# Neighbourhood attention: scores as four 64x64 tiles with 24 key columns each, instead of two 64x128 tiles with up to 32

## The chip, the cores and the metric

One core of a Trainium2 chip. The metric is the device time of one execution in microseconds. The kernel before takes 1035.6 us (median of three runs, 1035.43 to 1036.15).

## The reference

An encoder layer on 2048 tokens of width 1024, in float32: RMSNorm, one projection to q, k, v and a gate, neighbourhood attention, a SiLU gate, an output projection, the residual, and a final RMSNorm. The tokens form a grid of 32 rows by 64 columns; there are 16 heads of 64. Each query sees a window of 8 rows by 16 columns, clipped at the borders of the grid, with a learned bias per head and relative position. Cut to the attention:

```python
def row_fn(r):
    rs = jnp.clip(r - kh // 2, 0, rows - kh)
    qr = ...            # queries of row r, in blocks of 16 columns
    kr = ...            # keys of rows rs .. rs+7, 32 columns to a block
    s = jnp.einsum('bnqhd,bknjhd->bhnqkj', qr, kr) * scale
    s = jnp.where(col_valid[None, None], s + bias[None], NEG_INF)
    p = jax.nn.softmax(s.reshape(B, H, nb, NA_QBLOCK, kh * NA_KBLOCK), axis=-1)
    o = jnp.einsum('bhnqkj,bknjhd->bnqhd', p, vr)
```

## The kernel before

The program has one order, written out by hand; the order in which calls stand is the order on each engine. Stages one and two do the norm and most of the projections, by seven products instead of eight, with every float32 operand split in two parts (`h` and `l`, float32r). From about 573 to 929 us runs the attention, and after it the rest of the output projection (`rows_by_seven`).

The attention has 32 steps and one more for what is left over. A step is a pair of heads `p` and a row block `T` of 8 grid rows (512 queries); the list `order` has all eight pairs for `T` = 0, then `T` = 1 and 2 by turns, then all pairs for `T` = 3. The keys of a block are 11, 15, 15 and 12 grid rows (`KEY_ROWS`). The 512 queries are cut into four tiles `C` of 128: 8 rows by 16 columns, in two halves of 64 queries (8 rows by 8 columns). Tile `C` has its keys in strips of 8 columns. `KEY_COLS` gives three strips (24 columns) to the tiles at the edges, `C` = 0 and 3, and four strips (32 columns) to the inner ones. A half, by itself, reaches only three strips (its own and one on each side), and two at an edge of the grid.

In step `m` TensorE gets, one after another:

- `feed`: projection or output-projection matmuls, so many per step (`amount`), which fill the time of the other engines (L384, L386, L388; later L1481, L1483, L1485);
- `turns(m - 1)`: 44 transposes of 64 queries by one strip each (L1258, `ph`) of the normalised scores of the step before, into six PSUM banks that ACT and DVE copy to SBUF, three each (L1234, `pta`);
- `scores(2m)` and `scores(2m + 1)`: for each `C` two matmuls, one per head (L1173, `s`). The heads of a pair lie on 64 partitions each, so the two use different row halves of the array and different banks. Then, per `C` and head, DVE adds bias and mask and takes the row minimum (L1181), ACT takes the exponential and its sum (L1187), and `normalise` scales by the reciprocal on POOL (L1201), or on ACT for the last tile (L1199);
- `values(2m - 2)` and `values(2m - 1)`: 28 matmuls (L1280, `o`), one per `C`, strip and head, with the two heads on different column halves of the array.

All PSUM tiles come from one ring of eight banks. `strips(C)` lists for each strip which halves need it, and `places`, `turns` and `values` go by it, so strips of a half that sees nothing there are neither transposed nor multiplied with values.

The bias of a tile is a table per head: `load_e` loads a row of 15 x 32 positions per query, and `bias` adds the mask on POOL or DVE (L1141, `em`). For `T` = 3 the sum is made ahead and `load_last` loads it (L1156).

Of the kernel before, what the change touches and what calls it, by code (L numbers as in the profile page):

```python
# [10 lines left out]
F32 = mybir.dt.float32  # L11
F32R = mybir.dt.float32r
BF16 = mybir.dt.bfloat16
# [19 lines left out]
PLAIN = 6  # L33

KEY_ROWS = [(0, 11), (4, 19), (12, 27), (20, 32)]
KEY_COLS = [(0, 24), (8, 40), (24, 56), (40, 64)]
ROW_TYPE = [0, 1, 1, 2]
COL_TYPE = [0, 1, 1, 2]
TYPE_ROWS = [(0, 11), (-4, 11), (-4, 8)]
TYPE_COLS = [(0, 24), (-8, 24), (-8, 16)]  # L40
MASK_N = [[(u1 - u0) * (v1 - v0) for v0, v1 in TYPE_COLS] for u0, u1 in TYPE_ROWS]
MASK_ALL = sum(sum(n) for n in MASK_N[:2])
LAST_ALL = sum(MASK_N[2])
KINDS = {"q": 0, "k": 4, "v": 8, "g": 12}


def mask_table():
    out = []
    for t, (u0, u1) in enumerate(TYPE_ROWS):
        T = (0, 1, 3)[t]  # L50
        for c, (v0, v1) in enumerate(TYPE_COLS):
            C = (0, 1, 3)[c]
            half, qr, col, strip, kr, kc = np.ogrid[:2, T * 8:T * 8 + 8, :8, :(v1 - v0) // 8, T * 8 + u0:T * 8 + u1, :8]
            qc = C * 16 + half * 8 + col
            kc = C * 16 + v0 + strip * 8 + kc
            rs = np.clip(qr - KH // 2, 0, ROWS - KH)
            cs = np.clip(qc - KW // 2, 0, GW - KW)
            ok = (kr >= rs) & (kr < rs + KH) & (kc >= cs) & (kc < cs + KW)
            out.append(np.where(ok, 0.0, NEG).astype(np.float32).reshape(128, -1))
    return np.concatenate(out, axis=1)  # L60


def strips(C):
    out = []
    for s in range(KEY_COLS[C][0] // 8, KEY_COLS[C][1] // 8):
        halves = [h for h in range(2) if abs(2 * C + h - s) <= 1]
        out.append((s, s - KEY_COLS[C][0] // 8, halves[0] * 64, len(halves) * 64))
    return out


# [1 line left out]
def build(ctx, tc, x, xr, xt, wg, rpb, last, w_out, n0, nf, masks, out):  # L72
# [55 lines left out]
        nc.tensor.matmul(zp, z[:, :128], z, start=True, stop=True)  # L128
    ident = one.tile([128, 128], F32, name="ident")
    make_identity(nc, ident)  # L130
    ones = one.tile([128, 128], F32, name="ones")
    nc.vector.memset(ones, 1.0)
    onesr = one.tile([128, 128], F32R, name="onesr")
# [950 lines left out]
    def slot(T, p):  # L1084
        return 7 if p == lastp[T] else p - (p > lastp[T])

    def width(C):
        return KEY_COLS[C][1] - KEY_COLS[C][0]

    def load_k(p, T):  # L1090
        r0, r1 = KEY_ROWS[T]
        n = (r1 - r0) * GW
# [30 lines left out]
    def load_e(p, ty, pool_=None, homes=None):  # L1123
        r0, r1 = (4, 15) if ty == 0 else (0, 15)

        def rows(s):
            t = (homes[s] if homes else (pool_ or ep)([128, 512], F32, "e"))[:, :480]
            E[p, s] = t.rearrange("p (u v) -> p u v", v=32)
            nc.sync.dma_start(t[:, r0 * 32:r1 * 32], rpb[2 * p + s][:, r0 * 32:r1 * 32])

        return [lambda: rows(0), lambda: rows(1)]

    def bias(p, ty, cty):
        m0 = sum(sum(n) for n in MASK_N[:ty]) + sum(MASK_N[ty][:cty])
        (u0, u1), (v0, v1) = TYPE_ROWS[ty], TYPE_COLS[cty]
        n = MASK_N[ty][cty]
        sh = lambda a: a.rearrange("p (s u v) -> p s u v", u=u1 - u0, v=8)
        for s in range(2):
            t = mp([128, 512], F32, "em")[:, :n]
            EM[p, ty, cty, s] = t  # L1140
            (nc.gpsimd if attending[0] or not s else nc.vector).tensor_tensor(  # L1141
                sh(t), E[p, s][:, u0 + 4:u1 + 4, v0 + 8:v1 + 8].rearrange("p u (s v) -> p s u v", v=8), sh(MK[0][:, m0:m0 + n]), OP.add)

    def load_last(p):
        if p % 2:
            ts = [mp([128, 512], F32, "em") for _ in range(6)]
        else:
            m = mkp([128, 1536], F32, "em")
            e = [ep([128, 512], F32, "em") for _ in range(2)]
            ts = [m[:, :288], m[:, 288:576], m[:, 576:960], m[:, 960:1344], e[0], e[1]]  # L1150
        fs = []
        at = 0
        for cty, n in enumerate(MASK_N[2]):
            for s in range(2):
                EM[p, 2, cty, s] = t = ts.pop(0)[:, :n]
                fs.append(lambda t=t, a=at, n=n, s=s: nc.sync.dma_start(t, last[2 * p + s, :, a:a + n]))  # L1156
            at += n
        return fs

# [2 lines left out]
    def scores(i, between=None):  # L1162
        p, T, cs = pairs[i]
        kt, qt = KT[p, T], QT[p, T]
        r0, r1 = KEY_ROWS[T]
        got = []
        for C in cs:
            c0, c1 = KEY_COLS[C]
            qs = slice(C * 128, C * 128 + 128)
            pst = [bank((r1 - r0) * (c1 - c0), f"s{s}") for s in range(2)]  # L1170
            for s in range(2):
                a = slice(s * 64, s * 64 + 64)
                nc.tensor.matmul(pst[s], qt[a, qs], kt[a, :r1 - r0, c0:c1].rearrange("p r (s c) -> p s r c", c=8), start=True, stop=True)  # L1173
            got.append((C, pst))
        ST[i] = st = tiny.tile([128, 12], F32, name="st")
        for j, (C, pst) in enumerate(got):
            n = (r1 - r0) * width(C)
            X[i, C] = [xp([128, 512], F32, f"x{s}")[:, :n] for s in range(2)]
            for s in range(2):
                o = 2 * j + s  # L1180
                nc.vector.tensor_tensor_reduce(X[i, C][s], pst[s], EM[p, ROW_TYPE[T], COL_TYPE[C], s], -1.0, 1e38,  # L1181
                                               OP.add, OP.min, st[:, o:o + 1])
            if between and j == 0:
                between()
            for s in range(2):
                o = 2 * j + s
                nc.scalar.activation(X[i, C][s], X[i, C][s], AF.Exp, bias=st[:, o:o + 1], scale=-1.0,  # L1187
                                     accum_out=st[:, 4 + o:5 + o])
# [12 lines left out]
                    nc.gpsimd.tensor_scalar(X[i, C][s], X[i, C][s], st[:, o:o + 1], 1.0, op0=OP.mult, op1=OP.mult)  # L1201

    def split(C):
        return [b for b in strips(C) if b[3] == 128], [b for b in strips(C) if b[3] == 64]

    def places(m):
        p, T = order[m]
        put, at = {}, [1024, 1024]  # L1210
        for C in range(4):
            full, part = split(C)
            for b, blk in enumerate(full):
                for s in range(2):
                    for h in range(2):
                        put[C, blk[0], s, h] = C * 256 + b * 128 + s * 64
            for blk in part:
                for s in range(2):
                    h = blk[2] // 64
                    put[C, blk[0], s, h] = at[h]  # L1220
                    at[h] += 64
        return put

    def turns(m):
        p, T = order[m]
        k = 8 * (KEY_ROWS[T][1] - KEY_ROWS[T][0])
        put = places(m)
        PT[m] = t = pt([128, 3072], F32, "pta").rearrange("p (h c) -> p h c", h=2)
        banks_ = {}

        def copy(b):
            w = (512, 512, 384)[b]
            for h in range(2):
                (nc.vector.tensor_copy if h else lambda o, i_: nc.scalar.activation(o, i_, AF.Copy))(  # L1234
                    t[:k, h, b * 512:b * 512 + w], banks_[b, h][:k, :w])

        for b in range(2):
            for h in range(2):
                banks_[b, h] = bank(512, f"ph{h}")
            if b == 0:  # L1240
                banks_[2, 0], banks_[2, 1] = bank(384, "ph0"), bank(384, "ph1")
            lists = [[], []]
            for C in (2 * b, 2 * b + 1):
                full, part = split(C)
                for blks in (full, part):
                    for blk in blks:
                        for s in range(2):
                            for h in range(2):
                                if (C, blk[0], s, h) in put:
                                    lists[h].append((put[C, blk[0], s, h], C, s, blk[1] * k))  # L1250
            for h in range(2):
                lists[h].sort()
            for n in range(max(len(l) for l in lists)):
                for h in range(2):
                    if n < len(lists[h]):
                        o, C, s, at = lists[h][n]
                        q = slice(64 * h, 64 * h + 64)
                        nc.tensor.transpose(banks_[o // 512, h][:k, o % 512:o % 512 + 64], X[2 * m + b, C][s][q, at:at + k], ident[q, q])  # L1258
                if n == 7:
                    copy(b)  # L1260
        copy(2)

    def values(i):
# [8 lines left out]
        for C in cs:  # L1272
            X.pop((i, C))
            full, part = split(C)
            for b, (strip, _, q0, nq) in enumerate(full + part):
# [557 lines left out]
```

## Time and profile before

| | |
|---|---|
| median of 3 runs | 1035.6 us |
| profiled execution, its own time | 1035.7 us |
| its span | 1033.9 us |
| TensorE matmul busy | 1022.7 us, 99% of the span |
| weight loads | 838.6 us, 81% |
| DVE / ACT / POOL busy | 768.7 / 557.5 / 263.6 us |
| DMA | 221.04 MB, 214 GB/s on average |
| TensorE clock granted | 0.997 |
| score matmuls (L1173) | 512, 95.2 us busy |
| reductions (L1181) | 256, 123.0 us busy |

In rows of the profile, PE is TensorE's matmuls and PEld its weight loads, which run beside them. A row of the groups or of the timeline names the line, the operation, output and inputs, and the shapes; `64*128 64x480` on a matmul is 64 rows of the array by 128 of its columns, with 480 columns streamed through. The start of a matmul is measured, its end is modelled. The chain of waits lists the work that ended last, step by step, with start and duration. In a row of the windows, each engine has its busy time and, in brackets, its number of instructions.

### The profile page before, as it was taken

To read this page: it belongs to the slowest core of one execution; us is meant where nothing else is said; L and a number is where in the kernel's file an instruction comes from. 1 tells how busy PE (TensorE), PEld (TensorE's weight loads), DVE (VectorE), ACT (ScalarE), POOL (GpSimd) and SP (SyncE) were. 2 spreads that over 40 slices of the span, in tenths; PEclk is the share of its full clock that TensorE was granted. 3 is DMA by queue.
4 is the path that set the end of the run, shared out by engine and by line. 5 is a ranking of instruction groups with operands and counts; after the bars stand their busy time and mean duration, and the time that the engine had idled before them with its cause. 6 is when DMAs were issued, how large, how long until landed. Compare 5 with 4: busy or idle time off the path is not lost.

```text
span 1033.9 us, 20333 instructions
## 1 busy us (share of the span) xinstructions
PE 1022.7 (99%) x7208; PEld 838.6 (81%) x7208; DVE 768.7 (74%) x1650; ACT 557.5 (54%) x1305; POOL 263.6 (25%) x352
## 2 busy tenths in 40 slices
PE   9999999999999999999999999999999999999997
PEld 7888888887888888888888788888878788888875
DVE  5476878989898866776775756587787797777875
ACT  7645324353344423343343677688788778673432
POOL 0000231221221000000002467756566423321010
PEclk9999999999999999999999999999999999999998
DMA  9634667655636755755567788688776599899553
GB/s 315 234 102 140 191 179 244 187 194 170 204 99 201 250 152 164 222 189 179 193 205 237 215 236 244 199 250 290 237 246 225 177 300 315 255 349 372 134 153 102
DMA packets 143902, 221.04 MB, mean 214 GB/s; under 512 B 13176, under 2 KB 61560, under 8 KB 143800
## 3 DMA queue, kind: packets, MB, share of 16 engines
q1 hardware_dynamic: 141928, 216.72, 66.5%
q0 software_dynamic: 1440, 2.62, 1.6%
q8 instruction: 57, 0.93, 0.4%
q14 instruction: 45, 0.37, 0.1%
q10 hardware_dynamic: 432, 0.40, 0.1%
HBM read 154.68 MB, written 65.01 MB: 212 GB/s over the span
## 4 chain that ended last, share of the span: by engine, by line
PE 95%; DVE 3%; ACT 1%; issue 1%; DMA 0%; SPq 0%; DVEq 0%; ACTq 0%
PE pp L440 37%; PE py L1563 9%; PE pv L564 8%; PE s L1173 8%; PE o L1280 8%; PE pv L956 7%; PE ph L1258 4%; PE pp L386 2%; PE po L1481 2%; PE pp L388 2%; PE pp L384 2%; PE po L1483 2%; PE po L1485 2%; DVE f L423 1%; DVE x L1181 0%
## 5 line engine op out<-in xcount | busy, mean ns | idle before, releaser
L440 PE MATMUL pp<-h,f 128*128 128x512 f32 x672 | 217.3, 389 | 0.0
L1187 ACT ACTIVATE x<-x,st 128x360 f32<-128x360 f32 (+5 forms) x256 | 151.2, 592 | 24.3 <-DVE st L1181 24.3
L440 PEld LDWEIGHTS pp<-h,f 128*128 128x128 f32 x672 | 126.1, 188 | 26.1
L440 PE MATMUL pp<-t,f 128*128 128x512 f32 x558 | 141.7, 389 | 0.1
L1201 POOL TENSOR_SCALAR x<-x,st 128x480 f32<-128x480 f32 (+5 forms) x192 | 114.4, 613 | 93.9 <-DVE st L1192 91.5
L440 PE MATMUL pp<-l,f 128*128 128x512 f32 x336 | 130.7, 389 | 0.0
L460 POOL TENSOR_TENSOR tmp<-tmp,rb 128x512 f32<-128x512 f32 x36 | 59.0, 1640 | 267.6 <-DVE tmp L458 231.3
L1181 DVE CUSTOM_DVE_ANT_0 x<-s,em 128x360 f32<-128x360 f32 (+5 forms) x256 | 123.0, 535 | 0.8 <-PE s L1173 0.8
L440 PEld LDWEIGHTS pp<-t,f 128*128 128x128 f32 x558 | 104.7, 188 | 22.3 <-DVE u L453 0.6
L1141 POOL TENSOR_TENSOR em<-e,mk 128x264 f32<-128x264 f32 (+3 forms) x64 | 50.8, 824 | 248.4 <-DMA mk<-in_masks_dram 234.8
L423 DVE TENSOR_TENSOR f<-raw,f 128x512 fp32r<-128x512 f32 x105 | 75.2, 716 | 28.9 <-ACT f L422 28.5
L1173 PE MATMUL s<-kt,q 64*128 64x480 f32 (+5 forms) x512 | 95.2, 487 | 0.1
L1280 PEld LDWEIGHTS o<-pta,vt 120*64 120x64 f32 (+2 forms) x1792 | 80.9, 137 | 14.4 <-DVE st L1181 13.6
L1280 PE MATMUL o<-pta,vt 120*64 120x128 f32 (+5 forms) x1792 | 85.5, 253 | 0.5 <-DVE pta L1234 0.4
L422 ACT ACTIVATE f<-raw 128x512 fp32r<-128x512 f32 x105 | 63.6, 622 | 31.6 <-DMA raw<-in_wg_dram 13.9
L1173 PEld LDWEIGHTS s<-kt,q 64*128 64x128 f32 x512 | 65.1, 186 | 15.8 <-DVE pta L1234 1.9
L1234 DVE COPY pta<-ph 120x512 f32<-120x512 f32 (+5 forms) x96 | 56.9, 639 | 24.2 <-PE ph L1258 24.0
L440 PEld LDWEIGHTS pp<-l,f 128*128 128x128 f32 x336 | 63.1, 188 | 13.2
L1234 ACT ACTIVATE pta<-ph 120x512 f32<-120x512 f32 (+5 forms) x96 | 49.8, 557 | 37.4 <-PE ph L1258 36.6
L422 ACT ACTIVATE f<-s 128x512 fp32r<-128x512 f32 x42 | 26.3, 625 | 53.2 <-DVE s L429 49.5
L440 PE MATMUL pp<-sixths,f 128*128 128x512 f32 x198 | 54.6, 389 | 0.0
L1258 PEld LDWEIGHTS ph<-ident,x 64*120 64x120 f32 (+2 forms) x1408 | 42.5, 128 | 11.3 <-issue 8.5
(213 smaller groups left out, 1995.2 us busy)
## 6 DMA issues: line engine op xcount, KB each, us to landing
raw<-in_wg_dram SPq DMA_DIRECT2D x120, 256.0 KB, 5.0
row<-in_xr_dram SPq DMA_DIRECT2D x32, 256.0 KB, 5.7
vd<-v SPq DMA_DIRECT2D x32, 256.0 KB, 4.4
sgd<-sg SPq DMA_DIRECT2D x32, 256.0 KB, 2.8
q<-qd SPq DMA_DIRECT2D x32, 256.0 KB, 5.3
sgt<-sgd SPq DMA_DIRECT2D x32, 256.0 KB, 6.0
ogd<-og SPq DMA_DIRECT2D x32, 256.0 KB, 3.8
kt<-kd SPq DMA_DIRECT2D x16, 480.0 KB, 6.0
```

The lines of the kernel that those rows point to most:

```text
L422: nc.scalar.activation(t[:, 0], src, AF.Copy)
L423: nc.vector.tensor_tensor(t[:, 1], src, t[:, 0].bitcast(F32), OP.subtract)
L440: nc.tensor.matmul(B[n, P], t[:, int(m == 2), c], x[k][int(m == 1)], start=P in (1, 6, 5) and k == 0 and m == 0, stop=k == 3 and m == 2, s ...
L564: nc.tensor.matmul(ps[t], a[:, o], b, start=k == 0 and m == 0, stop=k == NK - 1 and m == 2)
L1173: nc.tensor.matmul(pst[s], qt[a, qs], kt[a, :r1 - r0, c0:c1].rearrange("p r (s c) -> p s r c", c=8), start=True, stop=True)
L1181: nc.vector.tensor_tensor_reduce(X[i, C][s], pst[s], EM[p, ROW_TYPE[T], COL_TYPE[C], s], -1.0, 1e38, OP.add, OP.min, st[:, o:o + 1])
L1187: nc.scalar.activation(X[i, C][s], X[i, C][s], AF.Exp, bias=st[:, o:o + 1], scale=-1.0, accum_out=st[:, 4 + o:5 + o])
L1201: nc.gpsimd.tensor_scalar(X[i, C][s], X[i, C][s], st[:, o:o + 1], 1.0, op0=OP.mult, op1=OP.mult)
L1234: (nc.vector.tensor_copy if h else lambda o, i_: nc.scalar.activation(o, i_, AF.Copy))(t[:k, h, b * 512:b * 512 + w], banks_[b, h][:k, :w])
L1258: nc.tensor.transpose(banks_[o // 512, h][:k, o % 512:o % 512 + 64], X[2 * m + b, C][s][q, at:at + k], ident[q, q])
L1280: nc.tensor.matmul(to.rearrange("d (h q) -> d h q", q=64) if nq > 64 else to, vt[:k, strip, s * 64:s * 64 + 64], t[:k, h, at:at + 64] if n ...
L1563: nc.tensor.matmul(B[m, P], t[:, a, c], b, start=P in (1, 6, 5) and k == 0 and i == 0, stop=k == 3 and i == 2, skip_group_check=True)
```

## The change

Every score tile becomes 24 key columns wide, counted from the half's own left neighbour strip. For each `C` and head there are now two matmuls, one per half of 64 queries, with the output on partitions 0 to 63 or 64 to 127 of the same bank. At the two edges of the grid one of the three strips does not exist: the matmul there has 16 columns, and a small bf16 matmul of zeros fills the other 8, so that the mask can work on defined numbers. The order in a `C` is: half 0 of head 0, half 0 of head 1, half 1 of head 0, half 1 of head 1, with a half's zeros ahead of it.

Masks, bias tables and the sums for `T` = 3 follow: 24 columns everywhere, the same three kinds of tile (left edge, inner, right edge). Reductions, exponentials and normalisation have 264, 360 or 288 elements for all tiles, where inner ones had 352, 480 or 384. Transposes and values keep their number and size and read at other offsets. The table loads have 24 columns instead of 32.

```diff
+    zeros = one.tile([128, 128], BF16, name="zeros")
+    nc.vector.memset(zeros, 0.0)
...
 def strips(C):
     out = []
-    for s in range(KEY_COLS[C][0] // 8, KEY_COLS[C][1] // 8):
+    for s in range(max(2 * C - 1, 0), min(2 * C + 3, 8)):
         halves = [h for h in range(2) if abs(2 * C + h - s) <= 1]
-        out.append((s, s - KEY_COLS[C][0] // 8, halves[0] * 64, len(halves) * 64))
+        out.append((s, halves[0] * 64, len(halves) * 64))
     return out
...
         for C in cs:
-            c0, c1 = KEY_COLS[C]
-            qs = slice(C * 128, C * 128 + 128)
-            pst = [bank((r1 - r0) * (c1 - c0), f"s{s}") for s in range(2)]
-            for s in range(2):
-                a = slice(s * 64, s * 64 + 64)
-                nc.tensor.matmul(pst[s], qt[a, qs], kt[a, :r1 - r0, c0:c1].rearrange("p r (s c) -> p s r c", c=8), start=True, stop=True)
+            pst = [bank((r1 - r0) * 24, f"s{s}") for s in range(2)]
+            R = (r1 - r0) * 8
+            for h in range(2):
+                g = 2 * C + h
+                j0, j1 = max(1 - g, 0), min(9 - g, 3)
+                q = slice(h * 64, h * 64 + 64)
+                for s in range(2):
+                    a = slice(s * 64, s * 64 + 64)
+                    if j1 - j0 < 3:
+                        j = 0 if j0 else 2
+                        nc.tensor.matmul(pst[s][q, j * R:j * R + R], zeros[a, :64], zeros[a, :R], start=True, stop=True)
+                for s in range(2):
+                    a = slice(s * 64, s * 64 + 64)
+                    nc.tensor.matmul(pst[s][q, j0 * R:j1 * R], qt[a, C * 128 + h * 64:C * 128 + h * 64 + 64],
+                                     kt[a, :r1 - r0, 8 * (g - 1 + j0):8 * (g - 1 + j1)].rearrange("p r (s c) -> p s r c", c=8),
+                                     start=True, stop=True)
             got.append((C, pst))
...
-            n = (r1 - r0) * width(C)
+            n = (r1 - r0) * 24
...
-            t = (homes[s] if homes else (pool_ or ep)([128, 512], F32, "e"))[:, :480]
+            t = (homes[s] if homes else (pool_ or ep)([128, 512], F32, "e"))[:, :360]
...
-                sh(t), E[p, s][:, u0 + 4:u1 + 4, v0 + 8:v1 + 8].rearrange("p u (s v) -> p s u v", v=8), sh(MK[0][:, m0:m0 + n]), OP.add)
+                sh(t), E[p, s][:, u0 + 4:u1 + 4].rearrange("p u (s v) -> p s u v", v=8), sh(MK[0][:, m0:m0 + n]), OP.add)
...
-                                lists[h].append((put[C, blk[0], s, h], C, s, blk[1] * k))
+                                lists[h].append((put[C, blk[0], s, h], C, s, (blk[0] - 2 * C - h + 1) * k))
```

More of the change, by code (lines that the diff above doesn't have):

```diff
@@ L35 @@
 KEY_ROWS = [(0, 11), (4, 19), (12, 27), (20, 32)]
-KEY_COLS = [(0, 24), (8, 40), (24, 56), (40, 64)]
 ROW_TYPE = [0, 1, 1, 2]
@@ L39 @@
 TYPE_ROWS = [(0, 11), (-4, 11), (-4, 8)]
[L40 to L43, printed above, removed]
+MASK_N = [(u1 - u0) * 24 for u0, u1 in TYPE_ROWS]
+MASK_ALL = 3 * sum(MASK_N[:2])
 KINDS = {"q": 0, "k": 4, "v": 8, "g": 12}
@@ L50, in mask_table @@
         T = (0, 1, 3)[t]
-        for c, (v0, v1) in enumerate(TYPE_COLS):
-            C = (0, 1, 3)[c]
-            half, qr, col, strip, kr, kc = np.ogrid[:2, T * 8:T * 8 + 8, :8, :(v1 - v0) // 8, T * 8 + u0:T * 8 + u1, :8]
+        for C in (0, 1, 3):
+            half, qr, col, strip, kr, kc = np.ogrid[:2, T * 8:T * 8 + 8, :8, :3, T * 8 + u0:T * 8 + u1, :8]
             qc = C * 16 + half * 8 + col
-            kc = C * 16 + v0 + strip * 8 + kc
+            kc = C * 16 + half * 8 - 8 + strip * 8 + kc
             rs = np.clip(qr - KH // 2, 0, ROWS - KH)
@@ L1085, in slot @@
         return 7 if p == lastp[T] else p - (p > lastp[T])
-    def width(C):
-        return KEY_COLS[C][1] - KEY_COLS[C][0]
     def load_k(p, T):
@@ L1126, in rows @@
         def rows(s):
-            t = (homes[s] if homes else (pool_ or ep)([128, 512], F32, "e"))[:, :480]
-            E[p, s] = t.rearrange("p (u v) -> p u v", v=32)
-            nc.sync.dma_start(t[:, r0 * 32:r1 * 32], rpb[2 * p + s][:, r0 * 32:r1 * 32])
+            t = (homes[s] if homes else (pool_ or ep)([128, 512], F32, "e"))[:, :360]
+            E[p, s] = t.rearrange("p (u v) -> p u v", v=24)
+            nc.sync.dma_start(t[:, r0 * 24:r1 * 24], rpb[2 * p + s][:, r0 * 24:r1 * 24])
         return [lambda: rows(0), lambda: rows(1)]
     def bias(p, ty, cty):
-        m0 = sum(sum(n) for n in MASK_N[:ty]) + sum(MASK_N[ty][:cty])
-        (u0, u1), (v0, v1) = TYPE_ROWS[ty], TYPE_COLS[cty]
-        n = MASK_N[ty][cty]
+        u0, u1 = TYPE_ROWS[ty]
+        n = MASK_N[ty]
+        m0 = 3 * sum(MASK_N[:ty]) + cty * n
         sh = lambda a: a.rearrange("p (s u v) -> p s u v", u=u1 - u0, v=8)
@@ L1149, in load_last @@
             e = [ep([128, 512], F32, "em") for _ in range(2)]
-            ts = [m[:, :288], m[:, 288:576], m[:, 576:960], m[:, 960:1344], e[0], e[1]]
+            ts = [m[:, :288], m[:, 288:576], m[:, 576:864], m[:, 864:1152], e[0], e[1]]
         fs = []
         at = 0
-        for cty, n in enumerate(MASK_N[2]):
+        n = MASK_N[2]
+        for cty in range(3):
             for s in range(2):
                 EM[p, 2, cty, s] = t = ts.pop(0)[:, :n]
-                fs.append(lambda t=t, a=at, n=n, s=s: nc.sync.dma_start(t, last[2 * p + s, :, a:a + n]))
+                fs.append(lambda t=t, a=at, s=s: nc.sync.dma_start(t, last[2 * p + s, :, a:a + n]))
             at += n
@@ L1203, in split @@
     def split(C):
-        return [b for b in strips(C) if b[3] == 128], [b for b in strips(C) if b[3] == 64]
+        return [b for b in strips(C) if b[2] == 128], [b for b in strips(C) if b[2] == 64]
     def places(m):
@@ L1218, in places @@
                 for s in range(2):
-                    h = blk[2] // 64
+                    h = blk[1] // 64
                     put[C, blk[0], s, h] = at[h]
@@ L1274, in values @@
             full, part = split(C)
-            for b, (strip, _, q0, nq) in enumerate(full + part):
+            for b, (strip, q0, nq) in enumerate(full + part):
                 for s in range(2):
@@ L1798 @@
     pad = pad.reshape(H, -1)
-    spread = np.stack([pad[:, (9 - r) * RPB_W + 7 - c:][:, :480] for h in range(0, 16, 8) for r in range(8) for c in range(h, h + 8)],
-                      axis=1)
+    spread = np.stack([pad[:, (9 - r) * RPB_W + 7 - c:][:, :480] for h in range(2) for r in range(8) for c in range(8)],
+                      axis=1).reshape(H, 128, 15, RPB_W)[:, :, :, :24]
     masks = mask_table()
     u0, u1 = TYPE_ROWS[2]
-    last, at = [], MASK_ALL
-    for (v0, v1), n in zip(TYPE_COLS, MASK_N[2]):
-        t = spread.reshape(H, 128, 15, 32)[:, :, u0 + 4:u1 + 4, v0 + 8:v1 + 8]
-        t = t.reshape(H, 128, u1 - u0, (v1 - v0) // 8, 8).transpose(0, 1, 3, 2, 4).reshape(H, 128, n)
-        last.append(np.where(masks[:, at:at + n] == 0, t, np.float32(NEG)))
-        at += n
+    t = spread[:, :, u0 + 4:u1 + 4].reshape(H, 128, u1 - u0, 3, 8).transpose(0, 1, 3, 2, 4).reshape(H, 128, -1)
+    last = np.where(masks[:, MASK_ALL:] == 0, np.concatenate([t] * 3, axis=2), np.float32(NEG))
     w = np.asarray(inputs["w_in_0"]).reshape(NK, 128, NU, 256).transpose(2, 1, 0, 3)
@@ L1816 @@
         "wg": np.ascontiguousarray(wg),
-        "rpb": np.ascontiguousarray(spread),
-        "last": np.ascontiguousarray(np.concatenate(last, axis=2)),
+        "rpb": np.ascontiguousarray(spread.reshape(H, 128, -1)),
+        "last": np.ascontiguousarray(last),
         "w_out": np.ascontiguousarray(np.asarray(inputs["w_out_0"])),
```

## The prediction

> **What bounds the kernel now.** I read the page's busy times first, then its chain, then the windows of the attention stage, and then single steps of that stage.
>
> ```profile
> span 1033.9 us, 20333 instructions
> PE 1022.7 (99%) x7208; PEld 838.6 (81%) x7208; DVE 768.7 (74%) x1650; ACT 557.5 (54%) x1305; POOL 263.6 (25%) x352
> PE pp L440 37%; PE py L1563 9%; PE pv L564 8%; PE s L1173 8%; PE o L1280 8%; PE pv L956 7%; PE ph L1258 4%; PE pp L386 2%; PE po L1481 2%; PE pp L388 2%; PE pp L384 2%; PE po L1483 2%; PE po L1485 2%; DVE f L423 1%; DVE x L1181 0%
> core 0: us, PE busy (x) PEld busy (x) DVE busy (x) ACT busy (x) POOL busy (x), PEclk, DMA share, GB/s
> 573.00:660.00 87.00, 87.00 (x996) 70.82 (x994) 57.19 (x190) 64.05 (x185) 58.85 (x99) 1.00 0.83 238
> 660.00:828.00 168.00, 167.87 (x2036) 136.74 (x2035) 126.62 (x372) 136.36 (x358) 96.89 (x139) 1.00 0.74 232
> 828.00:916.00 88.00, 87.91 (x1076) 71.74 (x1074) 71.01 (x232) 63.46 (x184) 28.34 (x48) 1.00 0.94 297
> ```
>
> TensorE is the bound. In the attention stage (573 to 916 us, the only part that this change touches) it has 0.2 us without work, at full granted clock. What shortens its list of work there shortens the kernel, until something else gets in its way. The chain shows how one of the 32 steps is made up; below it are one step each of row block 0 and of row block 3:
>
> ```profile
> 704.94 1.44 PE ph L1258 x44
> 706.38 3.00 PE s L1173 x16
> 709.38 2.60 PE o L1280 x56
> 711.97 0.43 PE pp L386
> 712.40 0.23 PE pp L388
> ...
> 619.73 2.42 PE s L1173 x15
> ...
> 903.66 2.56 PE s L1173 x15
> ```
>
> A step is transposes (ph), scores (s), values (o), then projection matmuls. The scores take 3.00 us in the 16 steps of row blocks 1 and 2, 2.42 in the 8 of block 0, 2.56 in the 8 of block 3. One of the 8 calls shows as two matmuls, two passes over the same columns, hence 16.
>
> **The change: columns on TensorE.** What does a pass cost?
>
> ```profile
> L1173 PE MATMUL s<-kt,q x8: 562/562/563, 716.8 to 718.2; 64*128 64x480 f32 x8
> L1173 PE MATMUL s<-kt,q x4: 462/462/463, 718.5 to 718.9; 64*128 64x360 f32 x4
> 772.03 0.52 PE L1173 MATMUL s<-kt,q 64*128 64x360 f32 x1
> 772.39 0.46 PE L1173 MATMUL s<-kt,q 64*128 64x360 f32 x1
> ```
>
> 120 columns more take 100 ns more: 0.833 ns a column, 0.30 us for 360. The last two rows are a step in which head 1 was held up, so head 0 streamed alone: 0.36 us from start to start, its first weight load included. A lone head is no faster than a pair. So the two heads, on the two row halves of the array, really run at once: per head 2 x (360 + 480 + 480 + 360) x 0.833 ns = 2.80 us, inside the 3.00. Blocks 0 and 3 give 2 x (264 + 352 + 352 + 264) = 2.05 and 2 x (288 + 384 + 384 + 288) = 2.24.
>
> After, each head's output is cut into two column halves of the array, one per 64 queries. Half 0 has 240 columns in the first tile (C = 0) and 360 in the other three; half 1 has 360 in three and 240 in the last. If all four tiles stream at once, each has 2 x 1320 x 0.833 = 2.20 us (block 0: 2 x 968, 1.61; block 3: 2 x 1056, 1.76). The floor falls by 0.60, 0.44 and 0.48 us a step. The first step has no transposes ahead; 4 x 88 columns fewer at 0.833 give it 0.3. All together 16 x 0.60 + 7 x 0.44 + 8 x 0.48 + 0.3 = 16.8 us: the most there is to gain.
>
> No row shows four tiles. But two row halves at once are shown above, and two column halves are the values: 32 passes of 128 columns and 24 of 64 would take 4.7 us one by one at 0.833, and 56 of them took 2.60. Four tiles of 64 x 64 write no more outputs per unit of time than the two score tiles do now, and read no more inputs than the two value tiles. I take four at once.
>
> **What then ends last.** The scores need PSUM banks that the transposes filled, and later a bank of their own:
>
> ```profile
> 706.21 3.17 PE L1173 MATMUL s<-kt,q 64*128 64x360 f32 x16
> 706.25 0.60 ACT L1234 ACTIVATE pta<-ph 120x512 f32<-120x512 f32 x1
> 707.82 0.08 DVE L1181 DVE_READ_ACCUMULATOR2_ANT st<- 128x1 f32 x1
> 708.91 0.46 PE L1173 MATMUL s<-kt,q 64*128 64x360 f32 x1
> 621.09 0.08 DVE L1181 DVE_READ_ACCUMULATOR2_ANT st<- 128x1 f32 x1
> 621.77 0.38 PE L1173 MATMUL s<-kt,q 64*128 64x264 f32 x1
> 905.03 0.08 DVE L1181 DVE_READ_ACCUMULATOR2_ANT st<- 128x1 f32 x1
> 905.82 0.40 PE L1173 MATMUL s<-kt,q 64*128 64x288 f32 x1
> ```
>
> Head 1's bank for the second C is free when the second ACT copy ends, at 706.85. I add 0.10 for wake-up and weight load (an estimate: a value matmul with its load takes 2.60/56 = 0.05). From there three C of 2 x 0.30 us end at 708.75. Before, the last pass started at 708.91 and streamed to 709.21. Gain 0.46, not 0.60.
>
> In block 0 the late bank is head 1's for the last C, which the first reduction (L1181) must leave: 621.09 + 0.08 + 0.10, then two passes of 264 (0.44) end at 621.71, against 621.77 + 0.22 = 621.99. Gain 0.28. In block 3: 905.03 + 0.18 + 2 x 0.24 = 905.69 against 906.06. Gain 0.37. In blocks 1 and 2 the same bank is free at 707.90, before the 708.15 at which that C begins.
>
> Sum: 16 x 0.46 + 7 x 0.28 + 8 x 0.37 + 0.3 = **12.6 us**.
>
> **What is added.** (1) A change of the array's split before the scores: today transposes and scores both use 64 rows by the full width. The price is the chain's first projection matmul after the values, 0.43 instead of 0.23: 0.20 us. (2) Four small bf16 matmuls a step that zero the 8 missing columns at each edge.
>
> ```profile
> 1.20 3.59 PE L128 MATMUL zp<-z 128*128 128x512 bf16 x8 [1.20 <-DVE z L125]
> 1.11 0.17 DVE L132 MEMSET ones<- 128x128 f32 x1
> 3.90 0.29 DVE L546 CAST wh<-raw 128x256 fp32r<-128x256 f32 x1 [2.62 <-DMA raw<-in_wg_dram]
> ```
>
> The only bf16 row: 0.45 us per 512 columns, so up to 0.11 for 120. They lie in the half that has 120 f32 columns fewer (0.20 for its two passes), and head 1's wait of 0.74 covers switch, zeros and the short first tile: 0.20 + 0.11 + 0.40 = 0.71 in half 0, and 0.20 + 0.60 = 0.80 in half 1, which then ends at 706.21 + 0.80 + 1.20 + 0.11 + 0.40 = 708.72, before 708.75. So both at nothing. Uncovered they are 31 x 0.31 = 9.6 us: the low end of the gain is 3. Below nothing they cannot go, being added work. (3) The memset of the zeros on DVE, at most the 0.17 of its larger neighbour, lies in DVE's 2.62 us wait for the first weights: nothing.
>
> The new matmuls wait for the same banks as the old; behind one that waits stand the rest of its C and then the values, as now. A reduction now waits for four score matmuls and perhaps a zeroing instead of two, but starts no earlier than the DVE copies end anyway. Transposes and values keep their count; only their offsets change.
>
> **Off the path.**
>
> ```profile
> L1181 DVE CUSTOM_DVE_ANT_0 x<-s,em 128x480 f32<-128x480 f32 x64 | 38.2, 653 | 0.0
> L1181 DVE CUSTOM_DVE_ANT_0 x<-s,em 128x360 f32<-128x360 f32 x64 | 30.9, 520 | 0.0
> L1181 DVE CUSTOM_DVE_ANT_0 x<-s,em 128x384 f32<-128x384 f32 x32 | 15.9, 549 | 0.0
> L1181 DVE CUSTOM_DVE_ANT_0 x<-s,em 128x352 f32<-128x352 f32 x32 | 14.9, 516 | 0.8 <-PE s L1173 0.8
> L1181 DVE CUSTOM_DVE_ANT_0 x<-s,em 128x288 f32<-128x288 f32 x32 | 13.3, 451 | 0.0
> L1181 DVE CUSTOM_DVE_ANT_0 x<-s,em 128x264 f32<-128x264 f32 x32 | 12.2, 418 | 0.0
> PEld ph L1258 <- POOL x L1201: 2.8, 8, 0.4
> ```
>
> All tiles are now as narrow as the edges were: DVE loses 64 x 0.133 + 32 x 0.098 + 32 x 0.098 = 14.8 us. Exponentials, normalising and the table sums shrink alike, and the table loads are a quarter smaller. None of it is on the path, but it decides whether the gain passes through: the next transposes need POOL's normalised scores, and that wait is in the list already. TensorE comes 0.46 us sooner, the last reduction 4 x 0.133 = 0.53 sooner, so the margin holds.
>
> **The skill against the trace.** The Trainium skill, "TensorE: Matmul & The Clock Gate", Part 3, says that weight loads overlap running matmuls only where the row group differs, and that matmuls keep program order; by that, half 1 would wait for half 0 and the sum be that of rival A. The value rows speak against it: their two tiles share all their rows and ran in 2.60 us instead of 4.7. "TensorEngine Tiling (Array Packing)", Key Properties, has the array drain when the tiling mode changes; the 0.43 agrees, and unhidden that rule alone would make the gain 12.6 - 6.2 = 6.4 us.
>
> **Rivals.** A (slower): the array carries only two f32 streams, and the halves run one after another. The scores then last 2 x 2.20 = 4.40 us plus 0.20 for the switch, against 3.00: +1.6; block 0 2 x 1.61 + 0.20 - 2.42 = +1.0; block 3 2 x 1.76 + 0.20 - 2.56 = +1.2. 16 x 1.6 + 8 x 1.0 + 8 x 1.2 = 43 us: 1079. It decides from the point where less than two thirds of one half lies beside the other (1.6 of 2.20 is what must overlap to break even). For it: no row has four tiles. Against it: both pairings are shown, each at full rate. B: a bf16 zeroing among f32 matmuls makes the whole array drain as a switch does, three more times a step, in the uncovered part: 31 x 0.60 = 18.6, less 12.6: +6, 1042; if only the last tile's pair counts, 31 x 0.40 = 12.4, 1036. No row joins bf16 to f32 in mid-stage. C: the gain of block 3 is lost, because DMA, at a share of 0.94 there, does not run 3% faster: 12.6 - 3.0 = 9.6, 1026. Against it: TensorE waits there for no DMA, and those loads shrink.
>
> **How the numbers follow.** Profiled run 1035.7 us (span 1033.9 and 1.8 around it), median 1035.6, so no correction. Likeliest: 1035.7 - 12.6 = **1023.1**, chance 0.72, own range 1019 (the floor) to 1032.7 (added work uncovered). C 0.07; B 0.07, half of it at 1036; A 0.14. The range 1019 to 1032 leaves out A, B and little more: about 0.2. A change of 0.2% is about what a measurement of this kernel can tell from none. Faster 0.80 (main, C and a little of B), same 0.04 (B at 1036), slower 0.16 (A, the rest of B).
>
> **What would show it.** Right: score matmuls of 64 x 64 with 240 and 360 columns, four in flight, score pieces in the chain of about 2.5 us in blocks 1 and 2, 2.1 in block 0 and 2.2 in block 3; L1181 near 108 us; values, transposes and projections as before. Wrong: half 1's matmuls starting only as half 0's end (A), gaps on both sides of the bf16 matmuls (B), transposes that start later after the projections on POOL or ACT (then the gain is given back), or score pieces shorter than 2.2 (then the bank waits are not what I think).

## The result and the profile after

The changed kernel takes 1023.81 us (median of four runs, 1023.56 to 1025.11), against 1035.81 us before (1035.43 to 1036.15): 12.0 us less, ratio 0.9887, 95% interval 0.987 to 0.9904. The profiled execution has a span of 1021.8 us, 12.1 below the 1033.9 before.

The page, busy times and chain by line:

```profile
span 1021.8 us, 21618 instructions
PE 1010.9 (99%) x7848; PEld 830.8 (81%) x7848; DVE 753.1 (74%) x1651; ACT 546.7 (54%) x1305; POOL 246.9 (24%) x352
PE pp L438 38%; PE pv L562 9%; PE pv L954 7%; PE o L1286 7%; PE py L1569 6%; PE s L1177 6%; PE ph L1264 4%; PE pp L384 2%; PE pp L386 2%; PE pp L382 2%; PE po L1487 2%; PE po L1489 2%; PE po L1491 2%; DMA t<-wodT 1%; DMA raw<-ogd 1%
```

TensorE is still the bound, with 640 more matmuls and 11.8 us less busy time. Line numbers have moved: scores L1173 are L1177 now (zeros L1174), reductions L1181 are L1187, exponentials L1193, normalising L1207, copies L1234 are L1240, transposes L1264, values L1286. The scores' share of the chain fell from 8% to 6%.

The chain in one step of row blocks 1 and 2, one of block 0 and one of block 3 (start, duration, what):

```profile
689.84 1.43 PE ph L1264 x40
691.27 0.17 PE s L1174 x2
691.44 1.95 PE s L1177 x25
693.39 0.01 PE s L1174
693.40 0.41 PE s L1177 x5
693.81 2.60 PE o L1286 x56
...
608.97 0.16 PE s L1174 x2
...
611.12 2.60 PE o L1286 x56
...
892.90 0.16 PE s L1174 x2
...
895.10 2.60 PE o L1286 x56
```

From the end of the transposes to the values, zeros and all: 693.81 - 691.27 = 2.54 us where it was 3.00; 611.12 - 608.97 = 2.15 where it was 2.42; 895.10 - 892.90 = 2.20 where it was 2.56. Transposes and values are as long as before.

For sums over all steps I use one measure below, the **score stage**: from the start of a step's last transpose to the start of its first value matmul, 31 steps, worked out from the traces. It went from 92.10 to 80.77 us, 11.3 of the 12.1 us of the span. The first step, which has no transposes, gives half of the rest: its two pieces of 1.24 us in the chain became 1.06 and 1.04, 0.38 less.

The timeline of TensorE in the narrow window 691.34 to 691.35 us, in the step shown first (a row gives the first start, the extent and the count of what was in flight), and then ACT's second copy and the first weight load after it:

```profile
691.30 0.53 PE L1177 MATMUL s<-kt,q 64*64 64x240 f32 x4
691.14 0.60 ACT L1240 ACTIVATE pta<-ph 120x512 f32<-120x512 f32 x1
691.79 0.19 PEld L1177 LDWEIGHTS s<-kt,q 64*64 64x64 f32 x4
```

The row stands under the shapes of its first matmul: two of the four have 240 columns (half 0) and two have 360 (half 1). They are in flight 0.04 us after the first of them started; in the trace their starts lie within 20 ns. ACT's second copy ends at 691.74. Head 1's second C begins 0.05 later; after its first pass (0.353) the passes follow each other every 0.302 us, and the sixth ends at 693.65. The values start 0.09 after that, as they do after the last score pass in all 31 steps of both kernels (the chain's 693.81 is the modelled end of that pass).

### The profile page after: what moved, and what is told of

It is laid out like the page before. It is cut to its first block, busy times and chain, and to the rows that moved or that the text cites. A ratio compares the mean times of both kernels' runs of the same rounds, so it can differ in the third digit from the quotient of the medians.

```text
span 1021.8 us, 21618 instructions
## 1 busy us (share of the span) xinstructions
PE 1010.9 (99%) x7848; PEld 830.8 (81%) x7848; DVE 753.1 (74%) x1651; ACT 546.7 (54%) x1305; POOL 246.9 (24%) x352
## 3 DMA queue, kind: packets, MB, share of 16 engines
q0 software_dynamic: 1440, 2.62, 1.6%
q8 instruction: 62, 1.02, 0.4%
## 4 chain that ended last, share of the span: by engine, by line
PE 91%; DVE 3%; DMA 3%; ACT 2%; issue 1%; DVEq 0%; ACTq 0%
PE pp L438 38%; PE pv L562 9%; PE pv L954 7%; PE o L1286 7%; PE py L1569 6%; PE s L1177 6%; PE ph L1264 4%; PE pp L384 2%; PE pp L386 2%; PE pp L382 2%; PE po L1487 2%; PE po L1489 2%; PE po L1491 2%; DMA t<-wodT 1%; DMA raw<-ogd 1%
## 5 line engine op out<-in xcount | busy, mean ns | idle before, releaser
L1193 ACT ACTIVATE x<-x,st 128x360 f32<-128x360 f32 (+2 forms) x256 | 139.8, 548 | 24.8 <-DVE st L1187 24.8
L1207 POOL TENSOR_SCALAR x<-x,st 128x360 f32<-128x360 f32 (+2 forms) x192 | 103.0, 554 | 93.6 <-DVE st L1198 91.3
L1187 DVE CUSTOM_DVE_ANT_0 x<-s,em 128x360 f32<-128x360 f32 (+2 forms) x256 | 108.9, 480 | 1.5 <-PE s L1177 1.5
L1136 POOL TENSOR_TENSOR em<-e,mk 128x264 f32<-128x264 f32 (+1 forms) x64 | 47.3, 769 | 248.5 <-DMA mk<-in_masks_dram 234.1
L1286 PEld LDWEIGHTS o<-pta,vt 120*64 120x64 f32 (+2 forms) x1792 | 80.9, 137 | 12.7 <-DVE st L1187 11.9
L1286 PE MATMUL o<-pta,vt 120*64 120x128 f32 (+5 forms) x1792 | 85.5, 253 | 0.5 <-DVE pta L1240 0.4
L1177 PE MATMUL s<-kt,q 64*64 64x360 f32 (+5 forms) x1024 | 76.9, 415 | 0.3 <-DVE pta L1240 0.3
L1240 DVE COPY pta<-ph 120x512 f32<-120x512 f32 (+5 forms) x96 | 56.7, 639 | 24.4 <-PE ph L1264 24.2
L1240 ACT ACTIVATE pta<-ph 120x512 f32<-120x512 f32 (+5 forms) x96 | 49.9, 557 | 36.7 <-PE ph L1264 35.9
L1177 PEld LDWEIGHTS s<-kt,q 64*64 64x64 f32 x1024 | 52.6, 132 | 11.6 <-DVE pta L1240 3.0
L1264 PEld LDWEIGHTS ph<-ident,x 64*120 64x120 f32 (+2 forms) x1408 | 42.3, 128 | 11.3 <-issue 10.2
```

The costliest lines, as they stand in the source:

```text
L1177: nc.tensor.matmul(pst[s][q, j0 * R:j1 * R], qt[a, C * 128 + h * 64:C * 128 + h * 64 + 64], kt[a, :r1 - r0, 8 * (g - 1 + j0):8 * (g - 1 + ...
L1286: nc.tensor.matmul(to.rearrange("d (h q) -> d h q", q=64) if nq > 64 else to, vt[:k, strip, s * 64:s * 64 + 64], t[:k, h, at:at + 64] if n ...
```

## The experiments

The theory is that of the prediction: the columns of each tile, and behind them head 1's late banks. Rivals: the gain comes from the work taken off DVE, ACT and POOL; the four tiles bring nothing over two narrower ones; the added zeros are on the path.

**The change again.** Run beside each set of experiments. In the first it took 1023.27 us against 1035.21 (ratio 0.9884, 0.987 to 0.9899, score stage 80.92), in the second 1024.61 against 1035.82 (0.9897, 0.9882 to 0.9912, score stage 80.75). The score stage repeats within 0.2 us, the time within about 1.5.

> The changed kernel again, beside the three that follow, so that they can be compared on one chip. Both theories: about 1023.8 us, ratio to the kernel before 0.988 to 0.990; from the last transpose to the first value matmul 2.70 us in row blocks 1 and 2, 2.30 in block 0, 2.35 in block 3.

> The changed kernel once more, beside the next three. About 1023.8 us.

**Only the other engines' work is cut.** The kernel before, with reductions, exponentials and normalising 24 columns wide, and the score matmuls as they were:

```diff
-            n = (r1 - r0) * width(C)
+            n = (r1 - r0) * 24
...
-nc.vector.tensor_tensor_reduce(X[i, C][s], pst[s], EM[p, ROW_TYPE[T], COL_TYPE[C], s], -1.0, 1e38,
+nc.vector.tensor_tensor_reduce(X[i, C][s], pst[s][:, :n], EM[p, ROW_TYPE[T], COL_TYPE[C], s][:, :n], -1.0, 1e38,
...
-                                    lists[h].append((put[C, blk[0], s, h], C, s, blk[1] * k))
+                                    lists[h].append((put[C, blk[0], s, h], C, s, min(blk[1], 2) * k))
```

It leaves out the fourth strip of the inner tiles; the transposes of that strip read the third again, so that their number stays. The table loads and the sums of tables and masks stay as wide as before.

> The kernel before with its score matmuls, but every reduction, exponential and normalisation only 24 columns wide; it leaves out the fourth strip of the inner tiles. Theory (TensorE's columns are the gain): DVE, ACT and POOL lose what the change took from them (L1181 from 123 to about 108 us), the score pieces stay at 3.00, 2.42 and 2.56 us, and the time stays at 1035.6 within 1 us. Rival (the gain came from the relieved DVE, ACT and POOL): most of the 12 us, 1025 to 1028.

1034.23 us against 1035.21, ratio 0.9988 (0.9978 to 0.9998). DVE lost the same 15 us as in the change (busy 753.3 against 753.1), and the chain's score pieces stayed. In its chain, a step of blocks 1 and 2:

```profile
693.27 1.45 PE ph L1258 x44
694.72 3.00 PE s L1173 x16
697.71 2.60 PE o L1280 x56
```

The score stage fell from 92.10 to 91.23; of those 0.87 us, 0.77 lie in two single steps, the 18th and the 24th of the 31 (3.66 to 3.26 and 3.08 to 2.70), and the rest is as it was. So lighter DVE, ACT and POOL are worth about 1 us of 12. The other 11 are not theirs; the next experiment shows what the fewer columns on TensorE bring.

**Two tiles of 24 columns.** The change with one matmul per head and C, 128 queries by 24 columns, and no zeros; so no change of the array's split before the scores either:

```diff
-            for h in range(2):
-                ...
+            c0 = 8 * min(max(2 * C - 1, 0), 5)
+            for s in range(2):
+                a = slice(s * 64, s * 64 + 64)
+                nc.tensor.matmul(pst[s], qt[a, C * 128:C * 128 + 128],
+                                 kt[a, :r1 - r0, c0:c0 + 24].rearrange("p r (s c) -> p s r c", c=8), start=True, stop=True)
```

> The changed kernel with two score matmuls per C again, 128 queries each, all 24 columns wide, no zeros, so no change of the column split ahead of the scores; it leaves out what lies in the fourth strip of the inner tiles. Theory (what counts is the columns streamed after head 1's late banks, 686 + 53 ns after the last transpose and then three C of 0.60 us): the same waits, a weight load of 128 columns instead of 64 behind each (about 0.05 us more), so 31 x 0.05 = 1.6 us more than the changed kernel, about 1025.4; 2.75, 2.35 and 2.40 us from transposes to values. Rival (four tiles at once are the gain in themselves): at most half of the 12 us is left, 1029 or more. Rival (column floors alone decide, 2 x 4 x 360 columns against 2 x 1320): +0.20 us a step in blocks 1 and 2, +0.15 and +0.16 in the others, 1028.5.

1026.69 us, ratio 0.992 (0.9903 to 0.9937). Its chain, in the same step as the first one of the change above:

```profile
689.85 1.43 PE ph L1254 x43
691.28 2.62 PE s L1168 x16
693.90 2.60 PE o L1276 x56
```

2.62 us, where four tiles with zeros and a switch of the split took 2.54. Here each head streams 2 x 4 x 360 columns, 2.40 us, and in the change 2 x 1320, 2.20. Over all steps the score stage is 82.23, 1.3 more than the change beside it, near the 1.6 expected. So of the 11.2 us that the stage lost beside this run, narrower tiles alone (with the lighter work of the other engines) bring 9.9, and four tiles instead of two the last 1.3. (These two tiles leave out the fourth strip of the inner ones; to have the right result with 24 columns, each half needs its own tile.)

The step from two tiles to four is as large as expected, 0.05 us in blocks 0 and 3 (2.35 and 2.40) and 0.05 to 0.07 in blocks 1 and 2 (2.75 to 2.76), and not the 0.15 to 0.20 of the column floors. The cause is the expected one too, a late bank and behind it a longer weight load (0.19 us for 128 columns, 0.13 for 64), except in seven steps of blocks 1 and 2. There head 1's second C starts 0.84 to 0.86 us after the last transpose, when its first is through, though its bank came free at 0.67 to 0.69; its own columns end last, by up to 0.02 us. That the number fits there too is luck.

The whole kernel is 3.4 us slower than the change, though. In the profiled executions the time from the first score matmul to the last value matmul differs by 1.2 us, as the scores do. After the attention, in work that the edit does not touch, two tiles took 107.0 us and the change 104.3; the trace of two tiles shows a granted clock of 0.91 between 940 and 960 us, where the change beside it has 1.00. So the rest lies outside the scores, and at least a part of it in the clock. That the tiles bring this clock about is not shown.

**Four times the zeros.** Each of the four zero matmuls of a step is issued four times, 12 more a step:

```diff
-                        nc.tensor.matmul(pst[s][q, j * R:j * R + R], zeros[a, :64], zeros[a, :R], start=True, stop=True)
+                        for _ in range(4):
+                            nc.tensor.matmul(pst[s][q, j * R:j * R + R], zeros[a, :64], zeros[a, :R], start=True, stop=True)
```

> The changed kernel with each zeroing matmul issued four times. Three more of about 52 ns in two tiles of C 0 and in two of C 3. Theory (hidden behind head 1's wait and in the half that is 120 columns shorter, with 0.07 to 0.09 us to spare in blocks 1 and 2): only what exceeds that shows, 0.09 us a step in blocks 1 and 2, 0.05 in the others, in all about 2 us, 1026. Rival (the zeroing lies on the path): 31 x 2 x 0.156 = 9.7 us, 1033.5. Rival (the array drains where bf16 and f32 meet): nothing beyond the theory, since the number of such joints stays, but then the changed kernel's trace has gaps of 0.1 us or more around them.

1027.14 us, ratio 0.9923 (0.9908 to 0.9938); score stage 84.09, 3.2 more than the change beside it, where I expected 2. Its chain, a step of blocks 1 and 2:

```profile
691.60 0.29 PE s L1175 x6
...
691.94 1.82 PE s L1178 x23
693.75 0.14 PE s L1175 x5
...
693.94 0.41 PE s L1178 x4
694.36 2.60 PE o L1287 x56
```

2.76 us instead of 2.54. In these steps the stage is 0.21 longer, in block 0 only 0.02 and in block 3 0.06. A zero matmul follows the one before it in its tile after 0.05 us, so three more are 0.15. I had counted them at the left edge, in half 0, where head 1's bank wait takes most of it in. The right edge decides. Half 1 waits for no late bank of its own. In the change its last pass ends before head 1's half 0 does by 0.01 us in seven steps of blocks 1 and 2 and by 0.07 in six others, and by 0.10 in blocks 0 and 3 (worked out from the traces). Here it ends 0.22 or 0.27 later in blocks 1 and 2, 0.13 in block 0 and 0.16 in block 3: it starts its first C later, behind more zeros, and has three more zero matmuls ahead of its last one. What exceeds the slack is what the stage grew by. So the cover over the added work is there, and in seven of the 16 steps that matter most it is used up to the last 0.01 us.

**The waiting tile first.** In the change, head 1's second C waits for ACT's second copy. If C = 1 is issued ahead of C = 0, the tile that gets the late bank is C = 0, which has 240 columns in one half, and less remains behind the wait:

```diff
-    pairs = [(p, T, (h, h + 1)) for p, T in order for h in (0, 2)]
+    pairs = [(p, T, cs) for p, T in order for cs in ((1, 0), (2, 3))]
...
-        if cs[0] == 0:
+        if cs[1] == 0:
```

> The changed kernel with the inner tile C = 1 ahead of the edge tile C = 0 in the first half of the scores; the rest in the same order, same result. Theory (in blocks 1 and 2 head 1's wait at 0.74 us after the last transpose ends last, because three full C stand behind it): now two full C and one with a short half stand behind it, all four tiles come to about 2.48 us, from transposes to values 2.57 instead of 2.70; blocks 0 and 3 end by the later wait for the first reduction and stay. 16 x 0.12 = 1.9 us faster than the changed kernel, about 1021.9. Rival (the column floor plus the switch of the split decides, not the banks): the floor is the same 2.20 us, so no change, 1023.8.

The stage of blocks 1 and 2 fell from 2.695 to 2.587 (2.57 expected) in 10 of 16 steps, and blocks 0 and 3 kept theirs (2.295, 2.347). Five others stood between 2.67 and 3.22, three of them above the change's own. The whole stage is 80.01, 0.75 less than the change; the time, 1024.69 us (ratio 0.9893, 0.9878 to 0.9908), does not tell it from the change's 1024.61. The chain shows the first and last piece of the scores in a good step and in a bad one, and DVE's timeline the cause; the first two DVE rows belong to the bad step, the last to the good one:

```profile
690.94 0.76 PE s L1177 x8
...
692.97 0.41 PE s L1177 x6
...
680.40 0.77 PE s L1177 x8
...
682.72 0.57 PE s L1177 x5
```

```profile
679.01 1.29 DVE L198 TENSOR_TENSOR wol<-raw,woh 128x512 fp32r<-128x512 f32 x2 [1.73 <-ACT woh L197]
680.22 1.75 DVE L1240 COPY pta<-ph 120x512 f32<-120x512 f32 x3
690.25 1.76 DVE L1240 COPY pta<-ph 120x512 f32<-120x512 f32 x3 [0.32 <-PE ph L1264]
```

The good step takes 2.44 us (692.97 + 0.41 - 690.94). In the bad one DVE comes to its three copies straight from splitting output weights (no idle time is shown before 680.22), and they end 1.57 us after the transposes (680.40) where those of the good step end 1.07 after them (690.94). The scores then wait for DVE's banks: 682.72 + 0.57 - 680.40, or 2.89 us. (The same step is a long one in the change too, with a stage of 2.89; here it is 3.03.)

The edit does two things in blocks 1 and 2. Head 1's second C no longer waits: its bank is free at 0.68 us after the last transpose, and its first C lasts until 0.80. And half 1 starts sooner, 0.16 us after the last transpose instead of 0.20 or 0.26, as no zeros stand ahead of it. So this run alone does not tell the bank from half 1's later start. The change's own trace does: half 1 starts at 0.20 and 0.26 in turns and ends 0.07 or 0.01 us before head 1's half 0, and yet the stage is 2.695 in both kinds of step. So the late bank decided there, as predicted, with half 1 close behind it; once the bank does not, half 1's own columns end last in the good steps (at 2.49 us after the last transpose), and DVE's copies in the bad ones.

**The third copy on ACT.** If ACT makes both halves' third copies, DVE has two, and the first reduction starts earlier:

```diff
-                (nc.vector.tensor_copy if h else lambda o, i_: nc.scalar.activation(o, i_, AF.Copy))(
+                (nc.vector.tensor_copy if h and b < 2 else lambda o, i_: nc.scalar.activation(o, i_, AF.Copy))(
```

> The changed kernel with both halves of the third copy of the transposes on ACT, none on DVE, so that DVE comes to the first reduction 0.45 us sooner; same result. Theory (blocks 0 and 3 end by head 1's bank for the last C, which the first reduction frees at 1.71 us): that bank is free at about 1.4, the other head's for the last C at about 1.60 when ACT's fourth copy ends, so the last C begins about 0.10 sooner; 2.20 and 2.25 us from transposes to values instead of 2.30 and 2.35; blocks 1 and 2 unchanged; 15 x 0.10 = 1.5 us faster than the changed kernel, about 1022.3. Rival (the banks do not decide): no change, or slower where ACT's exponentials come late.

1022.95 us, ratio 0.9885 (0.987 to 0.99), an interval that overlaps the change's; score stage 79.32, 1.4 less than the change. Block 0 fell from 2.296 to 2.215 (2.20 expected); blocks 1 and 2 stayed at 2.693, as they wait for ACT's second copy. Block 3 fell only from 2.347 to 2.335, where I expected 2.25. There head 1 came to its last C only 1.79 us after the last transpose, when its second and third C, begun behind ACT's second copy, were through; the bank was free before that. In block 3 the two waits lie almost level, and I had named only the one that came last. So the expected 1.5 came by another way, and that it did is luck: block 0 gave 0.56 us of the 1.4 and the usual steps of block 3 0.06; three single steps, in which DVE's copies had come late, gave 1.02, and the last step took 0.21 back.

**Both.**

> Inner tile first and the third copy on ACT together; same result. Theory: both gains, 1.9 + 1.5 = 3.4 us below the changed kernel, about 1020.4. Rival: 1023.8.

1020.46 us (1019.27 to 1021.3), ratio 0.9856 (0.984 to 0.9873), below the interval of the change beside it. Its chain, first piece of the scores and values, in a step each of blocks 1 and 2, 0, and 3:

```profile
689.80 0.77 PE s L1177 x8
...
692.24 2.60 PE o L1286 x56
...
608.70 0.62 PE s L1177 x8
...
610.70 2.60 PE o L1286 x56
...
878.86 0.65 PE s L1177 x8
...
880.97 2.60 PE o L1286 x56
```

2.44, 2.00 and 2.11 us, against 2.54, 2.15 and 2.20. The score stage is 76.56, 4.2 less than the change, where its two parts alone gave 0.75 and 1.4. The waits stand one behind the other: block 3 needs both (2.255 instead of 2.347), block 0 falls further than with the copy alone (2.150, where that gave 2.215), and with one copy fewer on DVE all but one of the steps of blocks 1 and 2 keep within 0.04 of 2.587. This version is the fastest of all that were run, 4 us below the change and 15 below the kernel before.

## Why the prediction was right

**Size.** 1023.1 was predicted and 1023.8 measured; 12.6 us of gain were predicted, and the span fell by 12.1. By the terms of the sum:

| term | predicted us | measured us |
|---|---|---|
| blocks 1 and 2, 16 steps | 16 x 0.46 = 7.4 | 7.0 (0.45 in most) |
| block 0, 7 steps | 7 x 0.28 = 2.0 | 1.9 (0.27) |
| block 3, 8 steps | 8 x 0.37 = 3.0 | 2.4 (0.36 in six) |
| first step | 0.3 | 0.4 |
| all else | 0 | 0.4 |

The usual step of each block came out within about 0.01 us, because the late bank and not the floor was taken for the end; the floors alone would have given 16.8. Where a term is short, it is mostly DVE's copies that came late: blocks 1 and 2 have one step that gained 0.26 for this reason (and one, the 18th of all, that gained 0.38; there ACT's first copy came late). The rest of block 3's term is two steps that gained 0.21 and 0.03. In the second of these DVE comes to its copies late in both kernels, behind the output projection's work, and the stage is 3.85 us before and 3.82 after:

```profile
849.15 1.29 DVE L1335 TENSOR_TENSOR gl<-ograw,gh 128x512 fp32r<-128x512 f32 x2 [2.08 <-ACT gh L1334]
850.36 1.41 DVE L1406 SCALAR_TENSOR_TENSOR y<-y,st,acc 128x512 f32<-128x512 f32 x2
851.68 1.74 DVE L1240 COPY pta<-ph 96x512 f32<-96x512 f32 x3
```

Quoting one step per block and multiplying missed that; with the third copy on ACT this step falls to 3.35.

**What ends last.** ACT's second copy to head 1's second C, and the first reduction to head 1's last C: taking away the first (the waiting tile first) shortened blocks 1 and 2 alone, freeing the second (the third copy on ACT) shortened the usual steps of block 0 by 0.08 and left those of blocks 1 and 2 as they were. For block 3 the step was half right, as above. Of the 0.10 taken for wake-up and load, the trace shows 0.05 before the first pass; the other 0.05 is in that pass, which takes 0.353 us where the next take 0.302.

**The rate.** Four tiles at once, each at 0.30 us per 360 columns: the passes of head 1 follow every 0.302 us while three other tiles stream. Rival A, halves one after another, falls: the starts of all four lie within 20 ns. By the rule of the Trainium skill, "TensorE: Matmul & The Clock Gate", Part 3 (a weight load overlaps only where the row group differs, and matmuls keep program order), half 1 would have waited for half 0. It does not, though it has the same 64 rows: with the zeros fourfold its first f32 matmul even starts 0.08 us ahead of half 0's, which stands before it in the program. In the change itself half 1 is the earlier by 0.02 us in the steps where it starts at 0.20. The measurement decides against the rule for tiles that differ in columns. (One support of the working was a little off: four tiles of 64 rows read 256 rows at a time and the two value tiles 240 in blocks 1 and 2, so more, and not "no more"; the full rate came all the same.)

**The added work, priced at nothing.** The three forms that the score matmuls have in blocks 1 and 2 of the changed kernel:

```profile
L1177 PE MATMUL s<-kt,q 64*64 64x360 f32 x384 | 40.6, 469 | 0.0
L1177 PE MATMUL s<-kt,q 64*64 64x240 f32 x128 | 19.0, 370 | 0.0
L1174 PE MATMUL s<-zeros 64*64 64x120 bf16 x64 | 7.6, 225 | 0.4 <-ACT pta L1240 0.4
```

In the step shown, half 0's f32 matmuls start 0.10 us behind the zeros, and at the right edge half 1's start 0.05 behind theirs, while the passes of half 0 go on beside them. TensorE sat idle before zeros for 0.4 us in all of the kernel. Rival B, 0.20 at each join, falls. The switch of the split shows as the first score matmul 0.146 us after the last transpose's start instead of 0.050 to 0.060 (0.051 to 0.058 with two tiles and no switch), so about 0.09, half of the 0.20 that I took. "TensorEngine Tiling (Array Packing)", Key Properties in the Trainium skill, has the array drain there, and the trace agrees, by these 0.09 us. Both are hidden, as the working had it, under head 1's wait in half 0 and by the shorter last tile in half 1. In blocks 1 and 2 half 1 was forecast to end 0.03 us before the late chain, and ends 0.01 or 0.07 before it. That this fits is in part luck: half 1 was to start 0.20 us later than the scores did before, for the switch alone. It starts 0.15 or 0.21 later, of which the switch is 0.09, and the rest goes with half 0's zeros, which stand ahead of it and which the working did not count there (without zeros ahead, in the experiment with the waiting tile first, it starts 0.11 later).

**Off the path.** Reductions in the forms of the changed kernel, and what weight loads waited for:

```profile
L1187 DVE CUSTOM_DVE_ANT_0 x<-s,em 128x360 f32<-128x360 f32 x128 | 59.9, 524 | 0.5 <-PE s L1177 0.5
L1187 DVE CUSTOM_DVE_ANT_0 x<-s,em 128x288 f32<-128x288 f32 x64 | 25.4, 450 | 0.0
L1187 DVE CUSTOM_DVE_ANT_0 x<-s,em 128x264 f32<-128x264 f32 x64 | 23.6, 421 | 1.0 <-PE s L1177 1.0
...
PEld s L1177 <- DVE pta L1240: 3.0, 8, 0.8
PEld ph L1264 <- POOL x L1207: 1.1, 3, 0.4
```

108.9 us, near 108. The transposes' wait for POOL, which could have given the gain back, fell from 2.8 us to 1.1. What grew is the scores' wait for DVE's copies, from 1.9 us to 3.0, which fits the missing tenths of blocks 1 to 3. Rival C had the place right, block 3, and the cause wrong: its term is 0.6 short where DVE's copies are late, and no wait for a DMA shows among the scores.

## What to carry to other kernels

Where matmuls are cut into more, smaller tiles of the array, count the columns of each tile as if it were alone, and then look for the buffer that comes free last: the second gave the number here, and the first would have promised a third more. A change that costs nothing because a wait covers it has used up that wait; multiply the added work in an experiment to see how deep the cover is. When one wait is taken away, ask what stands level with it: two changes worth 0.75 and 1.4 us of the stage alone were worth 4.2 together.

## What the runs showed of the hardware

- Matmuls of different tiles of the array do not hold each other's passes up: of two f32 matmuls on different tiles, the trace has first pass, first pass, second pass, second pass (691.30, 691.31, 691.52 and 691.56 us for half 0 of the two heads in the step shown), and a tile whose bank is late resumes by itself 0.05 us after its release while others stream.
- The order of matmuls of different tiles is not that of the program: half 1's first score matmul started before half 0's in the kernel with four times the zeros (0.296 and 0.381 us after the last transpose), and by 0.02 us in some steps of the change.
- A wait does hold up what stands behind it, on other tiles too: in the 18th step of the changed kernel head 1's zeros waited 0.6 us for an ACT copy, and head 0's score matmuls, whose bank was free, started only 0.1 us behind them.
- A bf16 matmul of 120 columns among f32 ones cost its tile 0.05 us (693.18 to 693.23 in the step shown); the 225 ns in its row hold the modelled end.
